# Weight and adaLN loads in halves: six slots of 4 KB a partition in place of three of 8 KB

## Chip, core and metric

The kernel runs on one core of a Trainium2 chip. The metric is the device time in microseconds of one execution; the time before is 2785.83 us, the median of three runs (2784.18 to 2786.69). Five engines work side by side: TensorE (PE, matrix products; PEld is its weight load), VectorE (DVE), ScalarE (ACT), GpSimd (POOL) and SyncE (SP, which here issues nearly all transfers between the chip's main memory and the on-chip buffer).

## The reference, cut to what matters

Two layers of a decoder over 256 tokens of width 2048, all in f32. Each layer has a token mixer and a SwiGLU block. Before each of these four sub-layers, the row c is turned into a shift, a scale and a gate (adaLN):

```
def _ada(c, w, b):
    mod = jax.nn.silu(c) @ w + b
    shift, scale, gate = jnp.split(mod, 3, axis=-1)
    return shift[:, None], scale[:, None], gate[:, None]
...
h = x * (1.0 + scale) + shift
y = mixer(h)        # or (silu(h @ wg) * (h @ wu)) @ wd
x = layer_norm(ALPHA * x + (1.0 + gate) * y)
```

The matrices w of adaLN are 2048 x 6144, one for each sub-layer: 201 MB in all, read once, for a product with a single row. The other weights (input and output projections of the mixers, gate, up and down matrices of the SwiGLU blocks) are multiplied with 256 rows. Layer 0 mixes with mLSTM and RWKV-7 heads, layer 1 with retention and gated DeltaNet heads.

## The kernel before

**Weights.** They lie in main memory as units of 1 MB: 128 partitions of 2048 f32, that is, four blocks of 128 rows by 512 columns side by side. `split` (line 688) loads a unit into one tile `raw` (line 683, pool `raw_p`, three slots of 8 KB a partition). It then treats the two halves of 1024 columns apart. For each half ACT makes `hi`, the value rounded to a shorter format (line 707), and DVE makes `lo`, the rest that `hi` leaves (line 708). `part` (line 712) multiplies both with the activations, three products for each pair, lines 722 to 724; a half feeds 12 products. `hi` and `lo` have three slots each. A slot of `raw` is free for the next load when the unit's second `lo` is done.

**adaLN.** The host has laid the adaLN matrices out in 192 units of 1 MB, 48 for a sub-layer. A unit holds 128 output columns as partitions, with the 2048 inputs along the row. `ada_unit` (line 634) loads one and lets DVE do one operation on it (line 644): the elementwise product with `silu(c)`, summed along the row into one column of `modulation`. After some units, small operations on DVE make the finished shift and scale from those columns, and after the 48th the gate. Units share the `raw` slots with the weights. In the first stage alone (`deep`) every second unit goes into a tile `a` of another pool instead: 16 of the 32 units of that stage.

**Order.** `first_products` (line 1279) starts with 32 adaLN units, since the first activations need them, and with weights that go into tiles `y` of yet another pool (`room`), not into `raw`. From then on `fill` (line 752) slips adaLN units in among the weight units at a rate for each stage: 1.5 per weight unit in the first mixer, 64/84 in the first SwiGLU block, less later, none towards the end.

**Who sets the order.** When the program is complete, the class `Plan` simulates it with a duration for each instruction (`cost`, line 289 on; an accumulating dot product counts 2373 ns, line 310) and a simple model of the transfers. Slots of a pool are given out in the order of the program. The order of each engine's instructions that comes out is imposed. SP's issues are part of it: they stand in one queue, and an issue whose slot is not yet free holds up those behind it.

Of the kernel before, what the change touches and what calls it, by code (L numbers as in the profile page):

```python
# [12 lines left out]
F32 = mybir.dt.float32  # L13
# [3 lines left out]
ALU = mybir.AluOpType  # L17
# [4 lines left out]
P = 128  # L22
# [189 lines left out]
class Plan:  # L212
# [82 lines left out]
    def cost(self, i):  # L295

        x, e = self.ins[i], self.eng[i]
        sizes = []
        for o in list(x.ins) + list(x.outs):
            if hasattr(o, "bass_ap"):  # L300
                n = 1
                for s, c in o.ap[1:]:
                    n *= int(c)
                sizes.append(n)
        n = max(sizes or [1])
        op = x.opcode
        if e == "DVE":
            if op == "TensorScalarPtr":
                if x.is_scalar_tensor_tensor:
                    d = 2373 if len(x.outs) > 1 or n >= 2048 else 150 + n * 1.045 + (55 if n > 100 else 5)  # L310
                elif x.is_tensor_tensor_scan:
                    d = 200 + n * 2.1
                else:
                    ptr = sum(1 for o in list(x.ins)[1:] if hasattr(o, "bass_ap"))
                    d = 145 + n * (0.77 if ptr else 0.55) + (100 if ptr and n > 100 else 0)
            elif op == "TensorCopy":
                ps = any(o.bass_ap.tensor.name in self.psum for o in x.ins if hasattr(o, "bass_ap"))
                d = 150 + n * (1.045 if ps else 0.53)
            else:
                d = {"BNStats": 135 + n * 1.07, "BNStatsAggregate": 168, "StreamShuffle": 179 + n * 1.1, "Memset": 60 + n * 0.5,  # L320
                     "Reciprocal": 157 if n < 64 else 150 + 2 * n}.get(op, 150 + n * 1.045)
            return max(d - 60, 15), d
        if e == "Activation":
            if len(x.outs) > 1:
                d = 500
            else:
                d = 200 + n * 0.83 + (80 if any(hasattr(o, "bass_ap") and k == 1 for o, k in zip(list(x.ins)[1:], sizes[1:])) else 0)
                d = d if n > 64 else max(300, d)
            return max(d - 60, 15), d
        if e == "Pool":  # L330
            d = {"TensorScalarAffineSelect": 1130 if n > 300 else 520, "TensorTensor": 1300, "TensorScalarPtr": 1000, "Memset": 100 + n}.get(op, 100)
            return d, d
        return 50, 50
# [196 lines left out]
class Trunk:  # L530
    def __init__(self, tc, ins, out, stack):
        self.tc, self.nc, self.ins, self.out = tc, tc.nc, ins, out

        def pool(name, bufs, **kw):
            return stack.enter_context(tc.tile_pool(name=name, bufs=bufs, **kw))

        self.fix = pool("fix", 1)
        self.raw_p = pool("raw", 3)
        self.split_p = pool("split", 3)
        self.h_p = pool("hp", 4)  # L540
        self.a_p = pool("ap", 5)
        self.y_p = pool("yp", 3)
        self.mix = pool("mix", 1)
        self.ps_g = pool("psg", 3, space=PSUM)
        self.ps_m = pool("psm", 3, space=PSUM)
        self.ps_c = pool("psc", 2, space=PSUM)
        self.dram = pool("scratch", 1, space=DRAM)
        self.n = 0
# [49 lines left out]
    def setup(self):  # L598
        nc, fix = self.nc, self.fix
        self.cols = fix.tile([P, NCOLS], F32, name="cols_sb")  # L600
        nc.sync.dma_start(self.cols[:], self.ins["cols"])
        self.cons = fix.tile([P, NCONS], F32, name="cons_sb")
        self.ident = self.con("ident")
        row = self.y8([P, D])
        nc.sync.dma_start(row[0:1, :], self.ins["crow"])
        ones = self.t1([P, P])
        nc.vector.memset(ones[0:1, :], 1.0)
        self.sc = fix.tile([P, D], F32, name="silu_c")
        for i, kind in enumerate("ccgg"):
            s = slice(512 * i, 512 * i + 512)  # L610
            b = self.bank(kind)
            nc.tensor.matmul(b[:], ones[0:1, :], row[0:1, s], start=True, stop=True)
            nc.scalar.activation(self.sc[:, s], b[:], AF.Silu)
        o = COLS["mu_r"][0]
        self.keep = fix.tile([P, 27], F32, name="one_less_mu")
        nc.vector.tensor_scalar(self.keep[:], self.cols[:, o:o + 27], -1.0, 1.0, ALU.mult, ALU.add)
        self.nkk = fix.tile([P, 16], F32, name="minus_kk")
        nc.vector.tensor_scalar(self.nkk[:, 0:8], self.cols[:, COLS["k_k"][0]:COLS["k_k"][0] + 8], -1.0, None, ALU.mult)
        nc.vector.tensor_scalar(self.nkk[:, 8:16], self.cols[:, COLS["k_a"][0]:COLS["k_a"][0] + 8], -1.0, 1.0, ALU.mult, ALU.add)
        self.rows = fix.tile([P, 32], F32, name="rows_sb")  # L620
        self.ab = fix.tile([P, 4, 32], F32, name="affine")
        self.mod = fix.tile([P, 48], F32, name="modulation")
        self.g1 = fix.tile([P, 16], F32, name="one_and_gate")
        self.ada_next = self.ada_pause = 0

# [8 lines left out]
    def ada_unit(self, u, deep):  # L634
        nc, v = self.nc, self.nc.vector
        sub, i = divmod(u, 48)
        src = self.ins["ada"][u]
        if deep and i % 2:
            w = self.a8([P, D])
            nc.sync.dma_start(w[:], src)  # L640
        else:
            w = self.raw(src)
        m = self.mod
        v.scalar_tensor_tensor(w[:], w[:], 1.0, self.sc[:], ALU.mult, ALU.mult, accum_out=m[:, i:i + 1])  # L644
        ob = COLS["adab"][0] + 48 * sub
        if sub == 0 and i < 32:
            if i % 8 in (5, 7):
                k = 4 * (i // 8) + i % 8 - 5
                j = i // 8 * 8 + i % 8 - 5
                v.tensor_tensor(self.ab[:, 0, 16 + k:18 + k], m[:, j:j + 2], self.cols[:, ob + j:ob + j + 2], ALU.add)  # L650
                v.scalar_tensor_tensor(self.ab[:, 0, k:k + 2], m[:, j + 4:j + 6], 1.0, self.cols[:, ob + j + 4:ob + j + 6], ALU.add, ALU.add)
            return
        if i < 32:
            if i % 8 < 7:
                return
            g = i // 8
            s = slice(4 * g, 4 * g + 4)
            sh, sc, bi = self.tiny([P, 4])[:], self.ab[:, sub, s], self.ab[:, sub, 16 + 4 * g:20 + 4 * g]
            v.tensor_tensor(sh, m[:, i - 7:i - 3], self.cols[:, ob + i - 7:ob + i - 3], ALU.add)
            v.scalar_tensor_tensor(sc, m[:, i - 3:i + 1], 1.0, self.cols[:, ob + i - 3:ob + i + 1], ALU.add, ALU.add)  # L660
            og, ol = COLS["lng"][0] + 16 * (sub - 1) + 4 * g, COLS["lnb"][0] + 16 * (sub - 1) + 4 * g
            v.tensor_tensor(bi, self.cols[:, ol:ol + 4], sc, ALU.mult)
            v.tensor_tensor(bi, bi, sh, ALU.add)
            v.tensor_tensor(sc, self.cols[:, og:og + 4], sc, ALU.mult)
            return
        if i == 47:
            v.scalar_tensor_tensor(self.g1[:], m[:, 32:48], 1.0, self.cols[:, ob + 32:ob + 48], ALU.add, ALU.add)

    def gate_rows(self, room, sub):
# [11 lines left out]


    def raw(self, src, room=None):
        w = room([P, 2048]) if room else self.raw_p.tile([P, 2048], F32, tag="raw", name=self.name("raw"))
        self.nc.sync.dma_start(w[:, :src.shape[-1]], src)
        return w

    def split(self, src, n, ahead=2000, homes="ss", room=None):


        nc = self.nc
        with self.tc.high_priority(offset=ahead):
            w = self.raw(src, room)
            parts = []
            for i, home in enumerate(homes):
                if home == "s":
                    hi = self.split_p.tile([P, 1024], F32R, tag="hi", name=self.name("hi"))
                    lo = self.split_p.tile([P, 1024], F32R, tag="lo", name=self.name("lo"))
                elif home == "a":
                    both = self.a8([P, 2, 1024], F32R)  # L700
                    hi, lo = both[:, 0], both[:, 1]
                elif home == "q":
                    hi, lo = (self.q4([P, 1024], F32R) for _ in range(2))
                else:
                    hi, lo = (self.own([P, 1024], "zt", 2, F32R) for _ in range(2))
                ws = w[:, 2 * n * i:2 * n * (i + 1)]
                nc.scalar.activation(hi[:, :2 * n], ws, AF.Copy)  # L707
                nc.vector.tensor_tensor(lo[:, :2 * n], ws, hi[:, :2 * n], ALU.subtract)  # L708
                parts.append((hi, lo))
# [1166 lines left out]
```

## Time and profile before

| | |
|---|---|
| median of three runs | 2785.83 us |
| span of the profiled execution | 2787.7 us |
| ScalarE busy | 1259.8 us |
| mean DMA rate over the span | 245 GB/s |
| loads of adaLN units into `raw`, into `a` | 176, 16 |
| adaLN dot products, DVE busy | 402.8 + 36.3 us |

The profiled execution's span is all that the page gives of its time; it lies 1.9 us above the median. In a row of the profile, `L708 DVE TENSOR_TENSOR lo<-raw,hi` is line 708 of the kernel, run by DVE, which wrote `lo` from `raw` and `hi`; what follows are shapes, the count, busy microseconds in all, the mean of one in ns, and the idle time of the engine before such instructions with what ended it. In the chain that ended last, `DMA raw<-gu` is the time from the issue of a load of `raw` to its landing.

### The profile page before, as it was taken

What the parts mean: (1) busy time and instruction counts of PE and PEld (TensorE: products, weight loads), DVE (VectorE), ACT (ScalarE), POOL (GpSimd) and SP (SyncE); (2) the same over time, 40 slices, a digit from 0 to 9 for tenths busy, and PEclk for the clock granted to TensorE, in tenths of its full rate; (3) what the DMA queues carried; (4) which work ended last, traced back from release to release, by engine and by line L of the source; (5) the groups of instructions that cost most, each with busy time, mean ns of one, the idle gap of its engine ahead of it and who ended that gap; (6) DMA issues with size and microseconds to landing.
All of it is one profiled execution on the core that took longest, in us unless ns stands there. A gap on an engine that the chain in (4) does not pass through costs nothing.

```text
span 2787.7 us, 33254 instructions
## 1 busy us (share of the span) xinstructions
PE 2660.5 (95%) x12618; PEld 2186.4 (78%) x12618; DVE 2019.5 (72%) x3189; ACT 1259.8 (45%) x1680; POOL 66.8 (2%) x88
## 2 busy tenths in 40 slices
PE   5698999999999999999999999999999999999997
PEld 3577778788787887788788888878778888888886
DVE  7899887768777467768777888885866646557557
ACT  2363445556543443434346545444454444443442
POOL 0000000110000000000000200000000000000000
PEclk8899999999999999999999999999999999999999
DMA  9978674325588578868856766675657656656554
GB/s 393 364 282 312 255 296 156 121 95 213 205 307 311 207 280 309 316 246 320 319 215 224 265 231 226 230 275 193 227 200 263 250 196 261 222 213 237 199 184 163
DMA packets 109818, 681.64 MB, mean 245 GB/s; under 512 B 12437, under 2 KB 15705, under 8 KB 31577
## 3 DMA queue, kind: packets, MB, share of 16 engines
q1 hardware_dynamic: 108506, 677.42, 66.3%
q8 instruction: 99, 1.62, 0.2%
q10 hardware_dynamic: 1152, 2.10, 0.2%
q14 instruction: 61, 0.50, 0.1%
HBM read 668.95 MB, written 10.52 MB: 244 GB/s over the span
## 4 chain that ended last, share of the span: by engine, by line
PE 71%; DMA 13%; DVE 11%; ACT 3%; issue 2%; POOL 0%; SPq 0%; DVEq 0%; ACTq 0%
PE g L723 20%; PE g L724 20%; PE g L722 20%; DMA raw<-ada 3%; DVE lo L708 3%; DVE raw L644 3%; DMA raw<-gu 3%; DMA a<-ada 2%; ACT hi L707 2%; DMA raw<-w_cd 1%; DMA raw<-w_ab 1%; PE m L1039 1%; PE m L1032 1%; PE m L1200 1%; PE m L967 1%
## 5 line engine op out<-in xcount | busy, mean ns | idle before, releaser
L708 DVE TENSOR_TENSOR lo<-raw,hi 128x1024 fp32r<-128x1024 f32 (+2 forms) x802 | 968.7, 1215 | 582.8 <-ACT hi L707 579.2
L707 ACT ACTIVATE hi<-raw 128x1024 fp32r<-128x1024 f32 (+2 forms) x802 | 837.6, 1051 | 1146.2 <-PE g L724 847.9
L722 PE MATMUL g<-hi,h 128*128 128x512 f32 (+2 forms) x2312 | 908.7, 395 | 49.6 <-ACT h L786 37.8
L723 PE MATMUL g<-lo,h 128*128 128x512 f32 (+2 forms) x2312 | 911.1, 394 | 10.1 <-DVE lo L708 9.5
L724 PE MATMUL g<-hi,h 128*128 128x512 f32 (+2 forms) x2312 | 908.1, 393 | 0.0
L722 PEld LDWEIGHTS g<-hi,h 128*128 128x128 f32 x2312 | 440.5, 191 | 145.9 <-ACT h L786 40.7
L723 PEld LDWEIGHTS g<-lo,h 128*128 128x128 f32 x2312 | 441.0, 191 | 107.5 <-DVE lo L708 21.1
L724 PEld LDWEIGHTS g<-hi,h 128*128 128x128 f32 x2312 | 441.0, 191 | 86.0 <-issue 2.0
L644 DVE SCALAR_TENSOR_TENSOR raw<-raw,silu_c 128x2048 f32<-128x2048 f32 x176 | 402.8, 2290 | 31.9 <-DMA raw<-ada 23.3
L722 PE MATMUL g<-hi,a 128*128 128x512 f32 x920 | 360.5, 392 | 4.0 <-DVE t L864 4.0
L723 PE MATMUL g<-lo,a 128*128 128x512 f32 x920 | 359.5, 391 | 2.6 <-DVE lo L708 2.6
L724 PE MATMUL g<-hi,a 128*128 128x512 f32 x920 | 359.7, 391 | 0.0
L722 PEld LDWEIGHTS g<-hi,a 128*128 128x128 f32 x920 | 173.2, 188 | 40.0 <-DVE t L864 4.4
L723 PEld LDWEIGHTS g<-lo,a 128*128 128x128 f32 x920 | 173.2, 188 | 38.5 <-DVE lo L708 3.4
L724 PEld LDWEIGHTS g<-hi,a 128*128 128x128 f32 x920 | 173.2, 188 | 35.9
L1382 DVE SCALAR_TENSOR_TENSOR f<-c,cols_sb,f 128x253 f32<-128x253 f32 (+2 forms) x120 | 56.2, 475 | 4.5 <-ACT f L1379 3.7
L1583 POOL TENSOR_SCALAR s<-cons_sb,log_alpha 128x128 f32<-128x128 f32 x16 | 13.7, 863 | 1035.5 <-DVE log_alpha L1527 886.8
L644 DVE SCALAR_TENSOR_TENSOR a<-a,silu_c 128x2048 f32<-128x2048 f32 x16 | 36.3, 2284 | 0.0
L906 ACT ACTIVATE t<-m,affine 128x128 f32<-128x128 f32 x96 | 34.9, 467 | 0.1
L970 ACT ACTIVATE a<-m 128x512 fp32r<-128x512 f32 x44 | 26.0, 591 | 14.8 <-PE m L967 13.6
L967 PE MATMUL m<-cons_sb,q 128*128 128x128 f32 x176 | 28.3, 285 | 3.6 <-DVE q L964 3.6
L707 ACT ACTIVATE hi<-y 128x1024 fp32r<-128x1024 f32 (+1 forms) x12 | 11.2, 937 | 44.5 <-DMA y<-w_ab 29.1
(448 smaller groups left out, 2120.3 us busy)
## 6 DMA issues: line engine op xcount, KB each, us to landing
raw<-ada SPq DMA_DIRECT2D x176, 1024.0 KB, 5.0
raw<-gu SPq DMA_DIRECT2D x176, 1024.0 KB, 5.2
raw<-dn SPq DMA_DIRECT2D x88, 1024.0 KB, 4.8
raw<-w_cd SPq DMA_DIRECT2D x60, 1024.0 KB, 4.9
raw<-w_ab SPq DMA_DIRECT2D x48, 1024.0 KB, 4.9
a<-ada SPq DMA_DIRECT2D x16, 1024.0 KB, 17.1
raw<-o_ab SPq DMA_DIRECT2D x16, 1024.0 KB, 4.8
raw<-o_cd SPq DMA_DIRECT2D x16, 1024.0 KB, 5.1
```

The lines of the kernel that those rows point to most:

```text
L644: v.scalar_tensor_tensor(w[:], w[:], 1.0, self.sc[:], ALU.mult, ALU.mult, accum_out=m[:, i:i + 1])
L707: nc.scalar.activation(hi[:, :2 * n], ws, AF.Copy)
L708: nc.vector.tensor_tensor(lo[:, :2 * n], ws, hi[:, :2 * n], ALU.subtract)
L722: mm(o, ah, wh, start=start and k == 0, stop=False)
L723: mm(o, ah, wl, start=False, stop=False)
L724: mm(o, al, wh, start=False, stop=stop and k == 3)
L906: nc.scalar.activation(h32[:, j, :], b[:, P * j:P * j + P], AF.Identity, bias=self.ab[:, sub + 1, 16 + k:17 + k], scale=self.ab[:, sub + 1 ...
L967: nc.tensor.transpose(b[:, P * k:P * k + P], gs[:, t, P * k:P * k + P], self.ident)
L1032: nc.tensor.matmul(x[:, 64 * j:64 * j + 64], mt[:, hs.start + j, :], dv[:, hs.start + j, :, 0, :], start=True, stop=True)
L1039: nc.tensor.matmul(x[:, 256 + 64 * j:320 + 64 * j], dt[:, hs.start + j, :], y[:, j, :], start=True, stop=True)
L1200: mm(b[:, T * x:T * x + T], bk[r, c, x, t, :], ar[r, c, t].rearrange("p x s -> p (x s)"), start=True, stop=True)
L1382: v.scalar_tensor_tensor(o[:, d:T], b[:, T * j:T * j + T - d], self.col(wname, 4 * (tile0 + i + j) + 3 - d), o[:, d:T], ALU.mult, ALU.add)
```

## The change

`raw_p` has six slots of 1024 columns (4 KB a partition) in place of three of 2048. Where `split` loads into `raw`, it does so for each half by itself, inside the loop over the halves; where it is given a `room`, it loads the whole unit as before. `ada_unit` loads and multiplies each half by itself and sums it into a column of its own: `modulation` has two planes, and `joined` adds them where the columns are first read, 24 more small operations in all. Units that go into `a` remain whole; their column in the second plane stays at the zero that is set at the start. In the plan's table an accumulating dot product counts by its length, 150 + 1.045 n + 85 ns, so 1305 ns for 1024 columns and 2375 for 2048.

```diff
@@ Plan.cost
-                    d = 2373 if len(x.outs) > 1 or n >= 2048 else 150 + n * 1.045 + (55 if n > 100 else 5)
+                    d = 150 + n * 1.045 + (85 if len(x.outs) > 1 else 55 if n > 100 else 5)
@@ Trunk.__init__ and setup
-        self.raw_p = pool("raw", 3)
+        self.raw_p = pool("raw", 6)
...
-        self.mod = fix.tile([P, 48], F32, name="modulation")
+        self.mod = fix.tile([P, 2, 48], F32, name="modulation")
+        nc.vector.memset(self.mod[:], 0.0)
@@ ada_unit
+        m, m2 = self.mod[:, 0], self.mod[:, 1]
         if deep and i % 2:
             w = self.a8([P, D])
             nc.sync.dma_start(w[:], src)
+            v.scalar_tensor_tensor(w[:], w[:], 1.0, self.sc[:], ALU.mult, ALU.mult, accum_out=m[:, i:i + 1])
         else:
-            w = self.raw(src)
-        m = self.mod
-        v.scalar_tensor_tensor(w[:], w[:], 1.0, self.sc[:], ALU.mult, ALU.mult, accum_out=m[:, i:i + 1])
+            for half, part in enumerate((m, m2)):
+                s = slice(1024 * half, 1024 * half + 1024)
+                w = self.raw(src[:, s])
+                v.scalar_tensor_tensor(w[:], w[:], 1.0, self.sc[:, s], ALU.mult, ALU.mult, accum_out=part[:, i:i + 1])
+
+        def joined(cols):
+            v.tensor_tensor(cols(m), cols(m), cols(m2), ALU.add)
+
...
+                joined(lambda x: x[:, i // 8 * 8:i // 8 * 8 + 8].rearrange("p (a b) -> p a b", a=2)[:, :, i % 8 - 5:i % 8 - 3])
...
+            joined(lambda x: x[:, i - 7:i + 1])
...
+            joined(lambda x: x[:, 32:48])
@@ raw
-        w = room([P, 2048]) if room else self.raw_p.tile([P, 2048], F32, tag="raw", name=self.name("raw"))
+        w = room([P, 2048]) if room else self.raw_p.tile([P, 1024], F32, tag="raw", name=self.name("raw"))
@@ split
-            w = self.raw(src, room)
+            if room:
+                w = self.raw(src, room)
             parts = []
             for i, home in enumerate(homes):
+                ws = w[:, 2 * n * i:2 * n * (i + 1)] if room else self.raw(src[:, 2 * n * i:2 * n * (i + 1)])[:, :2 * n]
...
-                ws = w[:, 2 * n * i:2 * n * (i + 1)]
```

## The prediction

> **What bounds the kernel now.** I read the page first (busy shares and the chain that ended last), then a table of stages, TensorE's waits, and the chain in the worst stage.
>
> ```profile
> span 2787.7 us, 33254 instructions
> PE 2660.5 (95%) x12618; PEld 2186.4 (78%) x12618; DVE 2019.5 (72%) x3189; ACT 1259.8 (45%) x1680; POOL 66.8 (2%) x88
> PE 71%; DMA 13%; DVE 11%; ACT 3%; issue 2%; POOL 0%; SPq 0%; DVEq 0%; ACTq 0%
> ```
>
> TensorE (PE) is busy 2660.5 of 2787.7 us. The change leaves its instructions alone, so it can take away only idle time, 127.2 us, and whatever a lower granted clock adds. The stages say where that idle time is (columns: stretch, length, busy us of each engine with its instruction count, granted clock, DMA share, GB/s):
>
> ```profile
> 0.00:140.00 140.00, 79.70 (x294) 62.27 (x295) 112.13 (x129) 45.74 (x63) 0.28 (x5) 0.84 0.94 378
> 140.00:210.00 70.00, 68.45 (x334) 53.09 (x333) 67.27 (x135) 45.16 (x82) 3.72 (x5) 1.00 0.77 281
> 210.00:280.00 70.00, 62.80 (x329) 51.30 (x328) 62.98 (x126) 26.20 (x36) 0.00 (x0) 0.93 0.82 310
> 280.00:350.00 70.00, 69.10 (x342) 53.38 (x341) 60.12 (x141) 33.14 (x62) 4.62 (x6) 1.00 0.71 259
> 350.00:420.00 70.00, 66.66 (x394) 54.97 (x392) 60.46 (x123) 30.84 (x58) 1.69 (x2) 0.95 0.77 287
> ...
> 2100.00:2300.00 200.00, 200.00 (x895) 165.55 (x894) 112.56 (x101) 87.20 (x91) 0.00 (x0) 1.00 0.65 236
> ```
>
> 60.3 us of it (140 − 79.70) lie in the first stage. From 140 to 420 PE idles 13.0 us while VectorE (DVE) is busy 250.8 of 280, and the second FFN leaves none. What ended PE's idle time (us in total, times, longest):
>
> ```profile
> PE g L722 <- ACT h L786: 47.1, 7, 13.5
> PE g L723 <- DVE lo L708: 12.1, 17, 2.3
> PE g L722 <- ACT hi L707: 10.4, 7, 3.3
> PE m L722 <- ACT hi L707: 9.5, 1, 9.5
> ```
>
> Asked for 140 to 2700 alone, the view gives the two middle rows unchanged, so the outer two are the first stage's. After it PE waits 12.1 + 10.4 = 22.5 us for the halves of a weight. That is the pool. The first stage itself waits for bytes; its chain of waits is one transfer after another, and the DMA engines are full:
>
> ```profile
> 7.36 19.22 DMA a<-ada
> ...
> 75.23 17.00 DMA y<-w_ab
> ```
>
> ```profile
> 20.00:30.00 10.00, 6.53 (x24) 5.56 (x24) 9.30 (x11) 4.07 (x6) 0.00 (x0) 1.00 1.02 420
> 30.00:40.00 10.00, 1.39 (x3) 0.67 (x4) 6.47 (x10) 2.00 (x2) 0.00 (x0) 0.67 0.97 394
> ...
> 90.00:100.00 10.00, 0.05 (x1) 0.05 (x1) 9.29 (x10) 3.73 (x5) 0.00 (x0) 0.57 1.01 418
> ```
>
> At 420 GB/s a 1 MB transfer takes 2.5 us, yet one needs 17 to 19 us to land, so some seven are under way at once. Smaller slots bring no byte sooner there. In the worst later stage the picture is another (chain from 200 to 260):
>
> ```profile
> by line: DMA raw<-w_ab 28.0%; DVE lo L708 19.7%; DVE raw L644 13.3%; DMA raw<-ada 9.8%; issue 8.4%; ACT hi L707 7.1%; DVE e L1013 2.4%; PE m L1039 1.5%; DVE z L1063 1.3%; DVE y L1017 1.0%; DVE e L1014 0.9%; DVE e L1015 0.9%; DVE y L1167 0.7
> ...
> 203.49 1.11 DVE lo L708
> 204.63 4.83 DMA raw<-w_ab
> 209.54 1.07 ACT hi L707
> 210.63 1.17 DVE lo L708
> ...
> 228.24 6.65 DMA raw<-w_ab
> 234.97 1.06 ACT hi L707
> ```
>
> A `lo` ends and frees a slot, the next 1 MB is issued, lands 5 to 7 us later, and only then its `hi` starts: the turnaround of three slots sets the pace, at 310 GB/s where 420 were to be had.
>
> **The change part by part.** *Loads in halves.* The loads into these slots, 588 by the page's list of DMA issues and nearly all of 1 MB, become 1176 of half the size. A half frees its slot after its own `lo`, not after the unit's second, and lands sooner:
>
> ```profile
> raw<-w_cd SPq DMA_DIRECT2D x60, 1024.0 KB, 4.9
> ...
> raw<-w_z SPq DMA_DIRECT2D x4, 512.0 KB, 3.4
> ```
>
> ```profile
> L685 SPq DMA_DIRECT2D raw<-gu x176: 327/328/333, 700.5 to 2682.4; - x176
> ```
>
> The first half is there 4.9 − 3.4 = 1.5 us earlier. A mean PE wait for `hi` is 10.4 / 7 = 1.5 us, so most of it goes: I take 8 of 10.4. The bounds are 0 (the next cause stands right behind) and 10.4. On SP's queue the change adds 588 issues of 0.33 us, 193 us over a span of 2788, on a queue that mostly stands waiting for a slot. Behind a waiting issue stand the residual blocks, the norm rows and the gate rows; each slot wait gets shorter, so I cost this at nothing. If that cover went, the second half of a unit would come 0.33 us later, with the first half's PE time (some 2.7 us, half of a unit's 24 matmuls at the 200 / 895 = 0.22 us of the row at 2100) to hide it. ScalarE's work stays: `hi` was made in halves before.
>
> *The adaLN dot product in two.* 176 operations of 2048 columns become 352 of 1024. No such half is in the trace; the nearest row is the `lo` of 1024 columns, also two f32 sources from SBUF:
>
> ```profile
> L708 DVE TENSOR_TENSOR lo<-raw,hi 128x1024 fp32r<-128x1024 f32 x786 | 957.4, 1225 | 577.3 <-ACT hi L707 573.8
> L644 DVE SCALAR_TENSOR_TENSOR raw<-raw,silu_c 128x2048 f32<-128x2048 f32 x176 | 402.8, 2290 | 31.9 <-DMA raw<-ada 23.3 <-ACT silu_c L613 7.5
> ...
> L644 DVE DVE_READ_ACCUMULATOR raw<-raw,silu_c 128x1 f32 x176 | 14.3, 82 | 0.0
> ```
>
> ```profile
> 15.95 2.28 DVE L644 SCALAR_TENSOR_TENSOR raw<-raw,silu_c 128x2048 f32<-128x2048 f32 x1
> ...
> 18.16 0.15 DVE L650 TENSOR_TENSOR affine<-modulation,cols_sb 128x2 f32<-128x2 f32 x1
> 18.24 2.28 DVE L644 SCALAR_TENSOR_TENSOR a<-a,silu_c 128x2048 f32<-128x2048 f32 x1
> ...
> 23.49 1.22 DVE L708 TENSOR_TENSOR lo<-y,hi 128x1024 fp32r<-128x1024 f32 x1 [0.26 <-ACT hi L707]
> ...
> 24.64 1.22 DVE L708 TENSOR_TENSOR zt<-y,zt 128x1024 fp32r<-128x1024 f32 x1
> ```
>
> Back to back, 2.21 us after the start of a 2048 (15.95) the next operation starts (18.16), and 1.15 us after that of a 1024 (23.49, 24.64): a unit costs 2 × 1.15 − 2.21 = 0.09 us more of DVE's time. By busy times, with nothing overlapped and a second accumulator read, it is 2 × 1.225 + 0.082 − 2.290 = 0.24 us. I take 0.09, since the short operations of the trace hide most of their length in the one before (0.15 us long, 0.08 us to the next start), and keep 0.24 for the range. A saving has no reason: the elements stay the same.
>
> In return a `lo` that comes ready behind an adaLN operation waits at most 1.2 us for it, not 2.3. The mean PE wait for `lo` is 12.1 / 17 = 0.7 us, about what a shorter operation in front can take away; not all of these waits are of that making, so I take half, 6 us, with bounds 0 and 12.1.
>
> What the 0.09 us costs depends on the stage (of this line alone, the count including accumulator reads, so two for a unit):
>
> ```profile
> 140.00:210.00 70.00, 25.85 (x22) 1.00 0.77 281
> 210.00:280.00 70.00, 27.52 (x24) 0.93 0.82 310
> 280.00:350.00 70.00, 23.26 (x21) 1.00 0.71 259
> 350.00:420.00 70.00, 24.77 (x22) 0.95 0.77 287
> ```
>
> From 140 to 420 run 89 / 2 = 44.5 units: 4.0 us. Of this I put 1.7 on the path, some 40%: `lo` and the dot product hold 33% of the chain between 200 and 260, smaller DVE lines the rest. Elsewhere 176 − 16 − 44.5 = 115.5 units give 10.4 us, of which DVE's 11% of the chain takes 1.1. In the first stage DVE is busy 112 of 140 us, so its 16 split units count in full, 1.4 us, with 8 of the 24 joining additions at 0.08 us (18.16 to the next start at 18.24), 0.6. The other 16 joins and the zeroing of 96 columns (before the first dot product, where DVE waited 7.5 us for `silu_c`) are under 1.5 us off the path.
>
> *Rows of 4 KB.* In the full first stage 16 units, 16.8 MB, now come as 4 KB rows: 40 us of transfer at 420 GB/s. The nearest row with short rows in it is 30 to 40 (394 GB/s; 2 KB rows of x and the 608 KB loads): 2.6 us if all went at that pace; shorter rows of the same bytes give full engines nothing to gain. I take 0, as the 16 units lie mostly in stretches like those at 20 and 90.
>
> *The plan* orders all engines anew with the new costs (a 1024 counts 1.3 us). That can shift anything by a few us either way; I take 0, with 4 us on both sides.
>
> **Sum.** −8 − 6 + 1.7 + 1.1 + 2.0 = −9.2 us, against the profiled span of 2787.7: 2778.5. The page gives no other time of that execution. The span is 1.9 us above the median shown, 2785.8, so the forecast for a median is 2776.6; its own range is 2766 to 2780.
>
> **The rivals.** *PE and the mixers were the bound anyway.* The waits for `hi` and `lo` are 0.8% of the span, and where one goes, another engine may be late a few hundred ns later: DVE is 90% busy in just the stage with the longest waits. Then gains of 3 to 5 us meet costs of 3 to 5: 2785. For it speaks the FFN row without idle time; against it the 310 GB/s of a slot-bound stage. Chance 0.31.
>
> *DVE becomes the bound from 140 on* (slower). From 140 to 210 it is busy 67.27 us beside PE's 68.45; 11 units at 0.24 us make 69.9 and pass PE, while at 0.09 they make 68.3 and do not. The point from which it decides is thus 0.11 us a unit. Priced at 0.24: 44.5 × 0.24 = 10.7, the first stage 16 × 0.24 + 0.6 = 4.4, the 4 KB rows 2.6, less some 8 us of waits that still go after 420: 9.7 us more, 2795. Against it: short operations overlap. Chance 0.14.
>
> *A fixed cost for each transfer* that isn't hidden (slower). By the two landing times, two halves in series take 6.8 us instead of 4.9; 16 units in the first stage pay 30.4, less the 14 gained later: 2802. Against it: seven transfers are under way at once and the engines are full. Chance 0.05. The Trainium skill (DMA: Bandwidth & Descriptors, Rules for kernel authors) asks for at least 1 MiB in a transfer for the most bandwidth; by its fit of 2.0 us plus bytes over 436 GB/s the 16 units would pay an estimated 32 us, which gives 2804. By that rule the change is wrong; here the rows at 20 and 90 show no such fixed part between transfers.
>
> *It doesn't do what it says*: the transfers in flight, not the slots, are the limit (some seven by the first stage). With halves that is 3.5 MB, still more than six slots hold, so it gives the first rival's 2785, within that chance.
>
> **How the numbers follow.** Forecast 0.50, first rival 0.31, the two slower ones 0.19. Within 0.2% (5.6 us) is about what a measurement of this kernel can't tell from no change; the forecast lies 9.2 below, the first rival inside, the others outside. The range 2764 to 2794 leaves the case of every wait gone (−22.5 + 4.8) and the transfers' fixed cost outside.
>
> **What would show it.** Right: the PE waits for `hi` and `lo` after 140 us fall from 22.5 us to under 10; 210 to 280 carries more than 310 GB/s and PE over 66 us; halves of the dot product take about 1.22 us; the first 140 us stay within 3. Wrong: halves over 1.3 us with DVE full from 140 to 280; under 410 GB/s between 20 and 100 us; or the waits gone and others (mixer tiles on DVE) in their place at the same span.

## The result, and the profile after

The changed kernel takes 2918.89 us (median of four runs, 2915.85 to 2929.29), the kernel before 2785.4 beside it: a ratio of 1.0478, 95% interval 1.0457 to 1.0499. It is 4.8% slower where 0.3% faster was forecast. The profiled execution spans 2914.0 us, 126.3 more than before.

First the page of the changed kernel (busy shares, and the chain that ended last by engine):

```profile
span 2914.0 us, 35337 instructions
...
PE 2697.0 (93%) x12618; PEld 2201.9 (76%) x12618; DVE 2031.5 (70%) x3566; ACT 1269.7 (44%) x1682; POOL 70.0 (2%) x88
...
PE 46%; DMA 20%; DVE 13%; issue 6%; ACT 3%; DVEq 0%; SPq 0%; ACTq 0%
```

PE runs the same 12618 products. It idles 217.0 us (2914.0 − 2697.0), 89.8 more than before; the other 36.5 us are PE busy for longer with the same work. Its mean granted clock is 0.973 in this execution and 0.981 in that of the kernel before; if busy time goes with the clock alone, that is an estimated 22 of the 36.5 us (2660.5 × 0.981 / 0.973 = 2682), and the rest wasn't pursued. VectorE is not the new bound: its busy share fell from 72 to 70%. In the chain PE's share fell from 71 to 46%, and what grew most is DMA, from 13 to 20%.

The waits of the changed kernel, PE's and then VectorE's own (us in total, times, longest). Line 719 now makes `hi`, 720 `lo`, 734 to 736 are the products, and 648 is the dot product on a half:

```profile
PE g L735 <- DVE lo L720: 58.0, 49, 3.7
PE g L734 <- ACT h L798: 47.6, 6, 16.1
PE g L734 <- ACT hi L719: 15.0, 5, 4.4
```

```profile
DVE lo L720 <- ACT hi L719: 446.3, 364, 3.3
DVE raw L648 <- DMA raw<-ada: 239.0, 118, 5.9
DVE t L867 <- DMA t<-x: 47.9, 17, 6.1
```

The first stage is as before (47.6 us for `h`, 47.1 then). PE's waits for `lo` and `hi` have gone from 22.5 to 73.0 us, 50.5 of the 89.8 us of new idle time; the rest is spread over smaller rows, the largest of them PE's wait for VectorE's `q` (3.6 to 14.5). And one of VectorE's own waits has grown out of all proportion: VectorE itself stands 239.0 us waiting for adaLN halves to land, where it stood 23.3. (The residual blocks `t<-x`, small loads in the same queue, are the same on a smaller scale: 47.9 us, 20.2 before.) The adaLN dot product isn't urgent, so this looks harmless, until one sees what stands behind it. Here is one such place (timeline of the changed kernel; start, length, instruction, and in brackets the idle time before it and what ended it):

```profile
1126.53 1.46 SPq L696 DMA_DIRECT2D raw<-ada  x2
...
1129.38 1.06 ACT L719 ACTIVATE hi<-raw 128x1024 fp32r<-128x1024 f32 x1 [2.01 <-PE g L736]
...
1133.24 1.23 DVE L648 SCALAR_TENSOR_TENSOR raw<-raw,silu_c 128x1024 f32<-128x1024 f32 x1 [4.46 <-DMA raw<-ada]
...
1135.62 2.36 DVE L720 TENSOR_TENSOR lo<-raw,hi 128x1024 fp32r<-128x1024 f32 x2
...
1136.89 0.50 PE L735 MATMUL g<-lo,h 128*128 128x512 f32 x1 [1.88 <-DVE lo L720]
```

A `hi` is ready at 1130.4. Its `lo` could run at once, for VectorE is idle. But in VectorE's fixed order two adaLN halves stand in front of it, and the first of them, issued at 1126.53, lands only 6.6 us later. VectorE idles 4.46 us, `lo` starts at 1135.6, over 5 us late, and PE stands 1.88 us. Whatever is held up also holds its slot, so the next load is issued late in its turn: behind this pair, SyncE waits 5.3 us with a half of `gu` until a dot product has freed a slot. The chain of this stretch is a circle: a load lands late, the dot products run late, and the slot that they free goes to the next load.

```profile
1126.53 6.62 DMA raw<-ada
...
1133.24 1.32 DVE raw L648 x3
...
1135.73 5.29 DMA raw<-ada
```

Why is an adaLN half so late? Landings by the two pages (count, size, median us from issue to landing), first the kernel before, then the changed one:

```profile
raw<-ada SPq DMA_DIRECT2D x176, 1024.0 KB, 5.0
raw<-gu SPq DMA_DIRECT2D x176, 1024.0 KB, 5.2
```

```profile
raw<-ada SPq DMA_DIRECT2D x352, 512.0 KB, 5.5
raw<-gu SPq DMA_DIRECT2D x352, 512.0 KB, 4.9
```

An adaLN half lands 0.5 us later than a whole unit did, a half of `gu` only 0.3 us sooner. The plan that fixes the order prices it otherwise. Its model of a transfer, which the change doesn't touch (times in ns; the rate is 358 bytes a ns):

```
dma = max(now + 500, dma) + by / self.rate
done[i] = max(dma + 1300, now + 2000)
```

For 1 MB alone this gives 0.50 + 2.93 + 1.30 = 4.73 us, a little under the 5.0 and 5.2 us that the trace of before shows. For 512 KB it gives 0.50 + 1.46 + 1.30 = 3.26 us, where the trace has 4.9 and 5.5: 1.6 to 2.2 us too early. The model lets transfers queue (`dma` carries over), so a half issued right behind another is planned later than 3.26; how far off the plan is on the mean was not worked out.

**Theory A** (order): the plan places adaLN halves in VectorE's order as if they were there 3.3 us after their issue; they aren't, and an engine that works in order stands. **Theory B** (transfer): 512 KB transfers are slow in themselves, and any order would starve. **Rival C** (VectorE): the second operation per unit costs the time. The kernel before ranges from 2775.96 to 2798.0 us over the runs below (0.8%), so each run is set against the kernel before on its own chip. Where one time stands against one, a difference of 10 us is not clear of that spread; those of 28 us and more are.

### The profile page after: what moved, and what is told of

Same layout as the page of the kernel before. It is cut to its first block, busy times and chain, and to the rows that moved or that the text cites. A ratio compares the mean times of both kernels' runs of the same rounds, so it can differ in the third digit from the quotient of the medians.

```text
span 2914.0 us, 35337 instructions
## 1 busy us (share of the span) xinstructions
PE 2697.0 (93%) x12618; PEld 2201.9 (76%) x12618; DVE 2031.5 (70%) x3566; ACT 1269.7 (44%) x1682; POOL 70.0 (2%) x88
## 4 chain that ended last, share of the span: by engine, by line
PE 46%; DMA 20%; DVE 13%; issue 6%; ACT 3%; DVEq 0%; SPq 0%; ACTq 0%
DMA raw<-ada 14%; PE g L735 14%; PE g L736 13%; PE g L734 13%; DVE lo L720 5%; DVE raw L648 3%; DMA t<-x 2%; ACT hi L719 1%; PE m L1051 1%; PE m L1044 1%; DMA raw<-dn 1%; DMA raw<-w_ab 1%; PE m L979 1%; DMA gate_row<-t 1%; DMA a<-gate_row 1%
## 5 line engine op out<-in xcount | busy, mean ns | idle before, releaser
L648 DVE SCALAR_TENSOR_TENSOR raw<-raw,silu_c 128x1024 f32<-128x1024 f32 x352 | 429.3, 1223 | 241.3 <-DMA raw<-ada 239.0
L867 DVE TENSOR_TENSOR t<-t,t 128x512 f32<-128x512 f32 x24 | 16.6, 691 | 48.0 <-DMA t<-x 47.9
L979 PE MATMUL m<-cons_sb,q 128*128 128x128 f32 x176 | 29.3, 294 | 14.5 <-DVE q L976 14.5
L979 PEld LDWEIGHTS m<-cons_sb,q 128*128 128x128 f32 x176 | 21.7, 148 | 22.2 <-DVE q L976 21.1
```

Of the source, the lines that this page charges most:

```text
L648: v.scalar_tensor_tensor(w[:], w[:], 1.0, self.sc[:, s], ALU.mult, ALU.mult, accum_out=part[:, i:i + 1])
L979: nc.tensor.transpose(b[:, P * k:P * k + P], gs[:, t, P * k:P * k + P], self.ident)
```

## Experiments

**e1: only the plan's price of a half.** 1.4 us later; everything else is the changed kernel. The edit goes by size, so it also moves the small loads under 600 KB, such as the residual blocks `t<-x` of 256 KB.

```diff
-                            done[i] = max(dma + 1300, now + 2000)
+                            done[i] = max(dma + (1300 if by > 600e3 else 2700), now + 2000)
```

> The changed kernel with one number altered: the plan now counts the landing of a transfer under 600 KB 1.4 us later (2.7 us after its bytes, not 1.3), so it expects a lone half 4.7 us after the issue instead of 3.3. Theory A (order): the changed kernel is slow because each engine's fixed order counts on halves landing after 3.3 us where the trace shows 4.5 to 5.5, so VectorE stands at the head of its queue waiting for an adaLN half (239 us) with finished weights' lo behind it. Then this edit takes most of the loss back: 2780 to 2815 us, VectorE's waits for adaLN halves under 80 us, PE's waits for lo under 25 us. Theory B (transfer): a 512 KB transfer itself is served at some 2 us when a few are queued, 260 GB/s, whatever the order. Then it stays above 2880 us and the waits move elsewhere.

2784.48 us, beside 2789.83 of the kernel before. One number in the plan takes back the whole loss. The waits of e1:

```profile
DVE raw L648 <- DMA raw<-ada: 91.8, 83, 4.9
...
PE g L735 <- DVE lo L720: 5.9, 12, 0.9
```

VectorE still waits 92 us, more than the 80 expected, but little of it reaches PE: its waits for `lo` are down from 58.0 to 5.9 us. VectorE's wait for `t<-x` is down too, from 47.9 to 15.9 us. B in its strong form has fallen.

**e2: only the dot product in two**, with slots and loads of 1 MB as before. Against the kernel before, cut to the dot product; the second plane, the additions and the plan's line for the shorter operation come with it:

```diff
             w = self.raw(src)
...
-        v.scalar_tensor_tensor(w[:], w[:], 1.0, self.sc[:], ALU.mult, ALU.mult, accum_out=m[:, i:i + 1])
+            for half, part in enumerate((m, m2)):
+                s = slice(1024 * half, 1024 * half + 1024)
+                v.scalar_tensor_tensor(w[:, s], w[:, s], 1.0, self.sc[:, s], ALU.mult, ALU.mult, accum_out=part[:, i:i + 1])
```

> The kernel before (three slots of 8 KB, loads of 1 MB) with only the adaLN dot product in two operations and the joins, in the plan's table too. Theories A and B both say that this part is not the cause: within 15 us of the kernel before (2786), halves of the dot product 1.22 us each. Rival C (VectorE): the second operation and its accumulator read are the loss; then 2850 us or more.

2800.49 us against 2789.83: 10.7 us more. C is no explanation of 133 us. This part is perhaps not free either: it is above the 4.8 us that the prediction gave it, though one run against one does not show that. A half takes 1220 ns on the mean, as foreseen.

**e3: only the loads in two**, two transfers into each 8 KB slot.

```diff
-        self.nc.sync.dma_start(w[:, :src.shape[-1]], src)
+        k = src.shape[-1]
+        if room:
+            self.nc.sync.dma_start(w[:, :k], src)
+        else:
+            for c in (slice(0, k // 2), slice(k // 2, k)):
+                self.nc.sync.dma_start(w[:, c], src[:, c])
```

> The kernel before with only the loads in two: each 8 KB slot is filled by two transfers of 512 KB, the dot product stays whole, the slots stay three. The plan expects the second half 4.7 us after the issue of the pair. Theory A: the halves land 1 to 2 us later than planned here too, so a part of the loss appears, 2800 to 2860 us. Theory B: every transfer takes 2 us, 4 us for a unit, and the stages with adaLN units starve: 2900 us or more. If neither smaller slots nor the order matter but only the dot product: 2786.

2817.97 us against 2789.83, 28.1 more: inside A's range, far from B's.

**m1: transfers by themselves.** It leaves the whole computation out: slots of a given size are filled and released again as soon as they have landed.

> Leaves the whole computation out: it streams rows of the adaLN array through 1, 2, 3, 4 or 6 slots of 1 MB or 512 KB, each released by a copy of one column, and writes zeros. It measures landing and rate by themselves. Theory A: halves in six slots move at least 380 GB/s, as 1 MB units in three do, and a lone half lands about 1.2 us before a lone 1 MB (3.6 against 4.8). Theory B: halves in six slots stay near 260 to 300 GB/s while 1 MB in three slots moves 380 or more.

The stages of m1 (columns: stretch, length, VectorE, GpSimd, clock, DMA share, GB/s), in the order 1 MB in one slot; 512 KB in one; 1 MB in two; 512 KB in two; in four; 1 MB in three; 512 KB in six; in three:

```profile
5.00:60.00 55.00, 1.69 (x11) 0.00 (x0) 1.00 0.66 230
65.00:150.00 85.00, 3.38 (x22) 0.00 (x0) 1.00 0.42 138
160.00:212.00 52.00, 3.23 (x21) 0.00 (x0) 1.00 1.00 405
222.00:310.00 88.00, 5.83 (x38) 0.00 (x0) 1.00 0.68 226
325.00:398.00 73.00, 7.06 (x46) 0.00 (x0) 1.00 0.93 335
410.00:460.00 50.00, 3.06 (x20) 0.00 (x0) 1.00 1.01 423
475.00:545.00 70.00, 7.72 (x51) 0.00 (x0) 1.00 0.97 376
560.00:620.00 60.00, 4.63 (x31) 0.00 (x0) 1.00 0.83 271
```

And landings, from the DMA issues of the first, the second and the fourth stage (1 MB in one slot, 512 KB in one, in two):

```profile
one_mb_x<-ada SPq DMA_DIRECT2D x11, 1024.0 KB, 4.7
```

```profile
half_x<-ada SPq DMA_DIRECT2D x22, 512.0 KB, 3.7
```

```profile
half_x<-ada SPq DMA_DIRECT2D x38, 512.0 KB, 4.6
```

This decides between order and transfer. Alone, a half lands after 3.7 us, a whole unit after 4.7. But with a second half under way it takes 4.6 us, and two halves in flight move 226 GB/s, no more than one whole unit does (230). In the changed kernel a half mostly has company: an adaLN unit's two are issued one behind the other, as at 1126.53, with weights before and behind. Against the plan's 3.26, a lone half lands 0.4 us later (3.7), one in company 1.3 (4.6). B keeps a remnant: six halves move 376 GB/s, just under the 380 that A expected, where three whole units move 423, 11% less. That is still above the 95 to 320 GB/s that the kernel before moves after its first stage (slices of the page).

**e5 and e6: which halves?** The plan is told of the later landing for adaLN halves alone (e5, shown), and for every other transfer under 600 KB (e6): the halves of the weights and, with them, the small loads.

```diff
-                            done[i] = max(dma + 1300, now + 2000)
+                            done[i] = max(dma + (2700 if by < 600e3 and str(ins[i].ins[0].bass_ap.tensor.name) == "ada" else 1300), now + 2000)
```

> The changed kernel; the plan counts only the adaLN halves' landing 1.4 us later, the weights' halves stay at the old 3.3 us. If the loss comes from VectorE standing in its queue before an adaLN half with lo behind it (theory A in its narrow form), this alone takes back most of the 126 us of span: 2785 to 2830. If it is halves of weights landing late before ScalarE's hi, it takes back little: above 2870.

> The counterpart: the plan counts only the weights' halves 1.4 us later, adaLN halves stay at 3.3 us. Narrow theory A: VectorE still stands before adaLN halves, 2850 to 2915. The other reading: 2785 to 2830.

e5: 2809.43 against 2775.96, 33.5 more than before. e6: 2873.7 against the same, 97.7 more. Of the 133.5 us of loss, the adaLN halves alone give back 100.0, the others 35.8. So the narrow reading carries three quarters. The last quarter goes with the weights' halves and the small loads, which e6 moves together: VectorE's wait for `t<-x` is 49.3 us in e5, as in the changed kernel, and 20.3 in e6, as before the change. Which of the two prices does it isn't separated. The waits of e5, then of e6, still those of the changed kernel:

```profile
DVE raw L648 <- DMA raw<-ada: 96.4, 77, 4.9
DVE t L867 <- DMA t<-x: 49.3, 17, 5.6
PE g L735 <- DVE lo L720: 11.4, 15, 1.7
```

```profile
DVE raw L648 <- DMA raw<-ada: 231.9, 125, 5.2
DVE t L867 <- DMA t<-x: 20.3, 16, 4.8
PE g L735 <- DVE lo L720: 47.6, 44, 3.2
```

**e9: e3 with the corrected price.** The same edit of the plan as e1, on e3.

> The kernel before with the loads in two (e3, 2818) and the plan's landing of a half 1.4 us later. Theory A: e3's loss of 28 us is of the same kind and goes, 2780 to 2800. If e3's loss is the price of 4 KB rows and twice the transfers in themselves, it stays at 2810 or more.

2776.57 against 2775.96, a little below A's range and far from 2810. e3's 28 us were of the same kind; twice the transfers and 4 KB rows cost nothing that this run shows.

**c2: the plan's error without the halves.** The kernel before, whole units and three slots, with the landing of every transfer planned 1.4 us earlier.

```diff
-                            done[i] = max(dma + 1300, now + 2000)
+                            done[i] = max(dma - 100, now + 2000)
```

> The kernel before, loads of 1 MB in three slots, with the plan's landing of every transfer 1.4 us earlier (a lone 1 MB at 3.3 us, traced 4.8): the error that the change brought in for halves, given to the old slots. Theory A: the loss comes with the error and not with the halves, 2820 us or more, with VectorE's waits for adaLN loads over 80 us (23 before). If the halves themselves are needed for the loss: within 10 us of the kernel before beside it.

2909.71 against 2797.5, 112 us more. The waits of c2:

```profile
DVE raw L644 <- DMA raw<-ada: 208.7, 104, 5.3
PE g L723 <- DVE lo L708: 73.0, 60, 3.9
```

The old kernel with the new error is nearly as slow as the new kernel, with the same two rows. A is shown from both sides: e5 takes most of the loss away by the adaLN price alone, c2 makes it without any half.

**e8, b1, b2, c1: what the slots are worth under a sound plan.** e8 and b2 count a half's landing 2.1 us later, b1 is e1 again, c1 the kernel before with every landing 0.7 us later (`dma + 2000`).

> The changed kernel with the plan's landing of a half 2.1 us later than in the change, against 1.4 in e1 (2784). The traced halves land 4.5 to 5.7 us after the issue, the plan then says 5.4 for a lone one. Theory A: once the plan isn't too early, more caution brings little: 2775 to 2800, VectorE's waits for adaLN halves below e1's 92 us.

> e1 again (the changed kernel, landing of a half 1.4 us later in the plan), timed in five rounds against the kernel before. One look gave 5.4 us less than the kernel before beside it. Theory A with a gain from finer slots left over: 0.998, interval below 1. If the finer slots bring nothing once the order is right: 1.000 within 0.002.

> e8 again (2.1 us later), timed. One look gave 4.7 us less than the kernel before beside it. Same two readings: 0.998, or 1.000 within 0.002.

> The kernel before with the plan's landing 0.7 us later for every transfer (a 1 MB load was planned at 4.7 us and traced at 4.8 to 5.2). A control: if a more careful plan alone is worth something, whatever the size of the slots, this too is some 5 us below the kernel before. If the plan of the kernel before was already right: within 4 us of it.

e8 gave 2771.27 against 2775.96, just below the range expected. In repeated runs, with the kernel before at 2786.95: b1 0.9986 (0.9968 to 1.0005), b2 **0.9949** (0.9932 to 0.9967), 2770.51 us, c1 0.9987 (0.9973 to 1.0001). b2's interval lies wholly below 1, by half a per cent; e8, the same program in one run, was 0.17% below. b1 and c1 can't be told from no change. The busy times of b2's page (its span is 2767.8 us), and its waits:

```profile
PE 2647.1 (96%) x12618; PEld 2184.6 (79%) x12618; DVE 2036.8 (74%) x3566; ACT 1270.3 (46%) x1683; POOL 70.1 (3%) x88
```

```profile
DVE raw L648 <- DMA raw<-ada: 34.4, 38, 5.5
...
PE g L734 <- ACT hi L719: 10.2, 8, 3.1
PE g L735 <- DVE lo L720: 4.6, 8, 0.9
```

PE's waits for `hi` and `lo` are 14.8 us now, below the 22.5 of the kernel before. All of the gain is in `lo` (12.1 to 4.6); the waits for `hi` are 10.2 beside 10.4. How much of b2's half per cent is the slots and how much mere caution isn't separated: c1 was cautious by 0.7 us, not by 2.1, and the kernel before with a larger margin wasn't tried. Nor with the later price for its small loads alone, which b2 moves too (VectorE's wait for `t<-x` is 8.4 us in b2, 5.2 in c1, 20.2 before).

## Why the prediction was wrong

- **The step that failed: "The plan orders all engines anew with the new costs … I take 0, with 4 us on both sides".** It cost some 112 to 139 us: 112 when the error is put into the old kernel, for every transfer (c2), 139 as the change's 133.5 less e1's −5.3, with the small loads priced later too. The prediction read the plan's price of the dot product, since the diff touched that line, and didn't ask what the plan thinks of a load whose size the diff halves. That price, 3.26 us, stood in the code; the trace of before had only four loads of that size, landing after 3.4 us, which seemed to bear it out.
- **The term beneath it: "The first half is there 4.9 − 3.4 = 1.5 us earlier".** The 3.4 us came from four transfers of 512 KB. Alone a half does land 1.0 us sooner (m1: 3.7 against 4.7), but among the others it lands after 4.9 to 5.5 us, so at most 0.3 of the 1.5 was there. With it went the −8 for `hi`: these waits rose to 15.0 us, and with the order put right they are 10.5 (e1) and 10.2 (b2) where 10.4 were.
- **−6 for `lo`.** Wrong in the change (12.1 became 58.0), by the plan. With the plan put right the waits fell to 5.9 (e1) and 4.6 (b2), which is the forecast size.
- **The residual blocks behind the slot waits, "I cost this at nothing".** VectorE's wait for them rose from 20.2 to 47.9 us. With e1's prices it is 15.9, so this too came by the order, not by the added issues.
- **VectorE, +4.8 in all.** The 1.15 us step and the 1.22 us of a half were right (1223 ns), and VectorE did not become the bound. The part alone costs 10.7 us in one run against one (e2), whose waits for `hi` and `lo` did not fall (27.8 us, 22.5 before). Which of its effects makes the difference wasn't pursued.
- **The first stage, 4 KB rows.** Right: from 20 to 100 us the changed kernel moves 423 GB/s, the kernel before 416 (first line).
- **The signs.** None of the three signs of a wrong forecast came up: the halves take 1.22 us, the first stage is over 410 GB/s, and the waits did not go. The signs of a right one failed: PE's waits rose, and 210 to 280 us carries 300 GB/s and 58.73 us of PE, less than before (second line).

```profile
20.00:100.00 80.00, 41.00 (x144) 32.99 (x144) 72.51 (x99) 22.24 (x29) 0.10 (x1) 0.78 1.02 423
...
210.00:280.00 70.00, 58.73 (x282) 46.96 (x282) 60.69 (x143) 24.97 (x33) 0.00 (x0) 0.95 0.89 300
```

- **The rivals.** The one that came nearest was the fixed cost for each transfer, at 0.05, and it stood in the wrong place: it was priced for the full first stage, where it is hidden. It showed in the thinly filled queue of the later stages, as landing time, and with an order that had been told of it (e9, b2) no loss is left. The Trainium skill's rule of at least 1 MiB in a transfer (DMA: Bandwidth & Descriptors, Rules for kernel authors) agrees with m1 at equal bytes in flight, 423 against 376 GB/s. It doesn't decide the case: b2 keeps the halves and is the fastest version here. The fit of 2.0 us plus bytes over 436 GB/s stands on that page for transfers issued by GpSimd; here SyncE issues them, and m1's lone transfers land after 3.7 and 4.7 us where it gives 3.2 and 4.4. The first rival, at 2785, is about where b1 stands. The rival with the plan's own error in it was not on the list.
- **The sum itself**, −9.2 us, is near what the change gives with later prices (−5.3 in e1, −4.7 in e8, half a per cent in b2), but that is partly luck. The term for `lo` was about right and the larger one for `hi` was not there. In b2's profiled execution PE idles 120.7 us beside 127.2 before (2767.8 − 2647.1 and 2787.7 − 2660.5), 6.5 less; the other 13.4 us between the two executions are PE's busy time, which was not forecast.
- **The range.** It was said to leave out the case of every wait gone, −22.5 + 4.8. From 2785.8 that case is 2768.1, which lies inside 2764 to 2794.

## What to carry to other kernels

Where a program fixes the order of in-order engines from a model, a change in the size of any transfer or operation is a change in what the model must know. Compare its price with the landing in the trace, for the size and the number in flight that the new version will have, before pricing anything else. Here a model that is a little late cost nothing that shows (b2 is better than b1), while one that is 1.4 us early cost 4% (c2). And an engine that is far from busy can still be the cause: look for what stands behind its waiting instruction.

## What the runs showed of the hardware

In m1, two transfers of 512 KB under way together moved 226 GB/s and landed after 4.6 us, one of 1 MB 230 GB/s after 4.7: at this depth, halving a transfer bought next to no time to landing. It takes four halves for 335 GB/s and six for 376, against 405 with two whole units and 423 with three. In the first stage, with more bytes queued, the changed kernel's mixture of halves and whole units ran at 423 GB/s, so the size alone didn't set the rate. The reason was not pursued.
